# One attention layer and a gated MLP in split fp32: steps of the hand-written order moved, low parts kept in spare tiles

## The chip, the cores and the metric

The kernel runs on one core of one Trainium2 chip. The metric is device time in microseconds (us) of one execution, as the median of several runs. TensorE (PE) multiplies; VectorE (DVE), ScalarE (ACT) and GpSimd (POOL) do everything element by element; SyncE (SP) only starts transfers (DMA).

## What is computed

One layer of a decoder on an input of 1024 tokens by 1024 features: a dilated sliding-window attention and then a gated MLP, each on a normalised input and added to it. Cut to what runs:

```python
h = rms_norm(x, mixer_norm)                       # (1024, 1024)
proj = (h @ w_in).reshape(1, 1024, 3, 3, 8, 64)   # 3 groups; q, k, v; 8 heads of 64
for g, (window, dilation) in enumerate(((128, 1), (512, 4), (2048, 16))):
    q = rms_norm(proj[:, :, g, 0], q_gain[g]) * 64 ** -0.5
    k = rms_norm(proj[:, :, g, 1], k_gain[g])
    o, lse = dilated_window_attention(q, k, proj[:, :, g, 2], window, dilation)
weights = softmax(stack(lses), axis=0)            # over the 3 groups
x = x + sum(weights * stack(outs)).reshape(1, 1024, 512) @ w_out
u = causal_depthwise_conv(rms_norm(x, ffn_norm) @ w_up, conv_w, conv_b)   # width 3, 5632 channels
gate, up = split(u, 2)
x = x + (silu(gate) * up) @ w_down                # 2816 -> 1024
```

## The kernel before

**Products.** Each fp32 product is made of three fp32r products: every operand is split into a high part (a cast to fp32r, nearly always on ACT) and a low part (the operand less its high part, on DVE or POOL), and PE adds high x high, high x low and low x high into one PSUM bank. So each operand costs PE nothing before it is used, but one cast and one subtraction on the other engines.

**Attention.** Tokens are normalised in 8 blocks of 128 (`Normed`, L96): squares on ACT, the root on POOL, the scaling on DVE (L107), then 8 transposes on PE (`turn`, L109) whose result is split into `hh` (high) and `hl` (low), tiles of 9 places of [128, 1024]. The attention then runs in six units (group, half of its heads) in the order (2,0), (2,1), (1,0), (1,1), (0,0), (0,1), each over 8 blocks of 128 tokens: blocks 0 to 47. A block has 8 projection steps, one for each 128 features (`project`, three matmuls of 512 columns into `qk`; `project_v`, three of 256 into `vp`), and behind them its norm (squares on ACT, sums on DVE, roots on POOL), the scaling of its heads, the values (`values`, L223), transposes and splits of its heads, scores, softmax, and the product with the values. A unit needs 8 weight tiles of [128, 768]: `load_raw` starts the transfer, `load_w` (L176) makes the high part on ACT and the low part on DVE (tiles 0, 2, 4, 5, 7) or POOL (1, 3, 6). There are 11 places for split weights, so tiles 0 to 2 of a unit are split during the unit before, and tiles 3 to 7 around its last block.

Each group wants the tokens in another order. At the two unit boundaries where the group changes (ahead of blocks 16 and 32), `reorder` (L126) copies the 8 feature tiles of `hh` (on ACT and DVE in turn) and of `hl` (on POOL) into the new order. Copy k writes the place that copy k-1 has read (`slot0`, 9 places for 8 tiles), so all of them stand behind the last projection steps of the last block of the unit. In the first of these changes a copy is made in two instructions, in the second in four.

The masks of groups 1 and 0 are made once (`make_masks`, L422): three POOL instructions for positions, two transposes on PE, five instructions on DVE.

**MLP.** `out_project` (L547) multiplies the attention output by `w_out` (split in halves by `split_wo`), adds the residual, and `norm2` (L559) normalises; its last line writes the row block to memory through SP's queue. `turn2` transposes the rows to PSUM; `turned` copies them to SBUF on ACT. w_up is multiplied by a scheme with seven products where plain blocks take eight: of rows of even and odd number and of four sums of them (`even`, `odd`), with X, Y, Z and V, sums of the blocks of w_up. `even` splits even row blocks (blocks 0, 2 and 4 from their copy in SBUF, with the low part on POOL, block 6 from PSUM on DVE), `odd` makes and splits the sums. The 22 pairs of gate and up columns (`Pair`) are loaded (`load`), split (`first` for X, `sums` and `second` for Y, `third` for Z, `fourth` for V), multiplied (`product`), convolved (`conv`: ACT scales, two instructions of DVE, L732, add the other taps) and gated. The down product follows with the same scheme.

**Order.** PE, ACT, DVE and POOL run their instructions strictly in the order in which the program issues them. For attention and MLP input, `at(t, f)` enters each step with a number t, and the steps are issued sorted by t; block i's projection step k stands at 8 i + k, and what follows the block at 8 i + 8 plus the entries of `T` (L35); N = 384 is where the output product begins, and `t` from L796 on is the start of the last row block. The numbers are an order, not a time. Behind the plan, the pairs are written out line by line from L901 on. SP is ordered by the framework: a transfer is issued about when its buffer comes free, in the order of the program.

Buffers that the change touches: the tag `wraw` in pool A (4 places of [128, 1024]), which holds in turn tokens, two raw weight tiles, the mask positions and, behind the attention, the raw `w_out`.

## Time and profile before

| | before |
|---|---|
| median of 3 runs | 1334.71 us (1334.53 to 1338.65) |
| the profiled execution | 1336.1 us, of which the profile's span 1334.2 |
| mean granted clock of PE | 0.992 |
| PE busy | 1284.2 us, 96% |
| DVE busy | 901.2 us, 68% |
| ACT busy | 616.0 us, 46% |
| POOL busy | 495.9 us, 37% |

The profile is of one execution; its times count from the start of the span. An engine's busy time counts its instructions without branches, semaphores and the issue of transfers. Attention runs from 0 to about 604 us, the output product and the input of the MLP to about 720, the pairs to about 1117, and the down product to the end. A wait is the idle time of an engine ahead of an instruction, with the instruction that released it. "Granted clock" (PEclk) is the share of its full clock that PE was given in a stretch.

### The profile page before, as it was taken

How to read it: one execution, taken by the hardware profiler on the slowest of the kernel's cores; microseconds unless marked ns; L12 is line 12 of the kernel's file. 1: busy time of each engine (PE TensorE's matmuls, PEld its weight loads, DVE VectorE, ACT ScalarE, POOL GpSimd, SP SyncE). 2: the span in 40 equal slices, each digit the busy share in tenths (PEclk: the TensorE clock that was granted, in tenths of full speed). 3: DMA queues.
4: the chain of work that ended last, by engine and by line, in shares of the span. 5: the costliest groups of instructions: out<-in, count | busy, mean ns of one | idle time of the engine just before them, and what ended most of it. 6: DMA issues, size and time to landing. Idle time of an engine off the chain costs nothing.

```text
span 1334.2 us, 19243 instructions
## 1 busy us (share of the span) xinstructions
PE 1284.2 (96%) x6911; PEld 1078.4 (81%) x6911; DVE 901.2 (68%) x1544; ACT 616.0 (46%) x1277; POOL 495.9 (37%) x599
## 2 busy tenths in 40 slices
PE   6999998999999999999988999999999999999998
PEld 4898887888878888887766788888888887888887
DVE  4665455454564565556776898888888888876664
ACT  4655354444454444435544444444444536444442
POOL 4333345333354555454533554454454443000000
PEclk9999999999998999999999999999999999999999
DMA  7112212112111121113721333323332328973341
GB/s 240 41 64 75 86 37 72 34 48 61 48 46 35 51 58 50 31 39 122 227 77 39 94 104 111 102 82 100 118 115 83 111 71 283 348 250 105 95 143 64
DMA packets 111614, 132.16 MB, mean 99 GB/s; under 512 B 6126, under 2 KB 80030, under 8 KB 111518
## 3 DMA queue, kind: packets, MB, share of 16 engines
q1 hardware_dynamic: 111518, 130.93, 30.7%
q8 instruction: 55, 0.90, 0.3%
q14 instruction: 41, 0.34, 0.1%
HBM read 95.91 MB, written 35.00 MB: 98 GB/s over the span
## 4 chain that ended last, share of the span: by engine, by line
PE 43%; DVE 3%; issue 2%; DMA 1%; POOL 1%; ACT 1%; SPq 0%; DVEq 0%; POOLq 0%; ACTq 0%
PE ua L687 15%; PE y L871 15%; PE uc L687 8%; PE ub L687 4%; DVE c L732 1%; DMA wB<-in_ffn_w_down 1%; POOL wxl L518 0%; DMA graw<-gde 0%; ACT c L730 0%; DVE sz L660 0%; DVE sy L656 0%; DVE c L743 0%; DVE bt L598 0%; POOL wyl L518 0%; POOL wzl L518 0%
## 5 line engine op out<-in xcount | busy, mean ns | idle before, releaser
L871 PE MATMUL y<-wd,g 128*128 128x512 f32 x924 | 210.4, 389 | 0.2
L871 PEld LDWEIGHTS y<-wd,g 128*128 128x128 f32 x924 | 173.4, 188 | 36.9 <-DVE wd L598 0.6
L198 PE MATMUL qk<-w,hh 128*128 128x512 f32 x384 | 159.0, 414 | 0.5 <-ACT hh L115 0.5
L199 PE MATMUL qk<-w,hh 128*128 128x512 f32 x384 | 153.5, 400 | 0.0
L200 PE MATMUL qk<-w,hl 128*128 128x512 f32 x384 | 152.6, 397 | 0.5 <-DVE hl L116 0.5
L79 POOL TENSOR_SCALAR ms<-ss 128x8 f32<-128x8 f32 (+1 forms) x64 | 12.9, 201 | 312.9 <-DVE ss L216 265.9
L207 PE MATMUL vp<-w,hh 128*128 128x256 f32 x384 | 122.8, 320 | 3.6 <-DVE v L228 3.6
L732 DVE SCALAR_TENSOR_TENSOR c<-uu,cw,c 128x1023 f32<-128x1023 f32 (+1 forms) x44 | 95.6, 2174 | 38.3 <-ACT c L730 37.5
L209 PE MATMUL vp<-w,hl 128*128 128x256 f32 x384 | 108.8, 283 | 0.0
L208 PE MATMUL vp<-w,hh 128*128 128x256 f32 x384 | 108.8, 283 | 0.0
L518 POOL TENSOR_TENSOR wyl<-sy,wyh 128x1024 fp32r<-128x1024 f32 x21 | 56.5, 2689 | 115.0 <-issue 61.0
L80 POOL TENSOR_TENSOR rs<-ms,half 128x8 f32<-128x8 f32 (+1 forms) x64 | 87.5, 1367 | 5.4
L207 PEld LDWEIGHTS vp<-w,hh 128*128 128x128 f32 x384 | 73.5, 192 | 18.5 <-DVE v L228 5.8
L314 ACT ACTIVATE sm<-sm,ust 128x128 f32<-128x128 f32 (+1 forms) x128 | 53.4, 418 | 76.0 <-DVE ust L311 73.4
L200 PEld LDWEIGHTS qk<-w,hl 128*128 128x128 f32 x384 | 73.3, 191 | 18.7 <-DVE hl L116 1.2
L267 ACT ACTIVATE qT<-tr,gains 128x256 fp32r<-128x256 f32 x48 | 22.7, 473 | 134.8 <-PE tr L256 134.8
L216 DVE TENSOR_REDUCE ss<-qn 128x8 f32<-128x512 f32 x48 | 32.9, 685 | 75.8 <-ACT qn L214 75.8
L208 PEld LDWEIGHTS vp<-w,hh 128*128 128x128 f32 x384 | 73.6, 192 | 9.3
L270 DVE SCALAR_TENSOR_TENSOR qT<-tr,gains,qT 128x256 fp32r<-128x256 f32 x48 | 23.2, 484 | 85.5 <-ACT kT L269 85.5
L518 POOL TENSOR_TENSOR wxl<-uraw,wxh 128x1024 fp32r<-128x1024 f32 x22 | 58.4, 2653 | 44.8 <-ACT wxh L517 44.7
L198 PEld LDWEIGHTS qk<-w,hh 128*128 128x128 f32 x384 | 74.0, 193 | 1.1 <-ACT hh L115 0.9
L199 PEld LDWEIGHTS qk<-w,hh 128*128 128x128 f32 x384 | 74.1, 193 | 0.1
(186 smaller groups left out, 3363.0 us busy)
## 6 DMA issues: line engine op xcount, KB each, us to landing
uraw<-in_ffn_w_up SPq DMA_DIRECT2D x44, 512.0 KB
raw<-in_attn_w_in SPq DMA_DIRECT2D x48, 384.0 KB
wB<-in_ffn_w_down SPq DMA_DIRECT2D x44, 256.0 KB
graw<-gds SPq DMA_DIRECT2D x44, 256.0 KB
gdo<-c SPq DMA_DIRECT2D x11, 512.0 KB
...
```

What stands on the lines that cost most here:

```text
L80: nc.gpsimd.tensor_tensor(r[:, :n], t[:, :n], half[:, :n], op=ALU.pow)
L198: nc.tensor.matmul(self.qk, a, w[:, 0, :512], start=k == 0, stop=False)
L199: nc.tensor.matmul(self.qk, a, w[:, 1, :512], start=False, stop=False)
L200: nc.tensor.matmul(self.qk, b, w[:, 0, :512], start=False, stop=k == KT - 1)
L207: nc.tensor.matmul(self.vp, a, w[:, 0, 512:], start=k == 0, stop=False)
L208: nc.tensor.matmul(self.vp, a, w[:, 1, 512:], start=False, stop=False)
L209: nc.tensor.matmul(self.vp, b, w[:, 0, 512:], start=False, stop=k == KT - 1)
L314: nc.scalar.activation(sm[:, h, lo:], sm[:, h, lo:], AF.Exp, scale=-1.0, bias=st[:, 256 + h:257 + h], accum_out=st[:, 260 + h:261 + h])
L518: eng.tensor_sub(l, raw, h.bitcast(F32))
L687: nc.tensor.matmul(acc[:, lo:hi], w[z][:, s + k], a[y][:, j, k, lo:hi], start=begin and lo == 0 and k == 0 and n == 0, stop=k == 3 and n == 2,
L732: nc.vector.scalar_tensor_tensor(c[:, k:], u[:, :S - k], cw[:, 2 - k, j:j + 1], c[:, k:], op0=ALU.mult, op1=ALU.add)
L871: nc.tensor.matmul(y, gs[:, z, ts], ws[:, w], start=f and n == 0, stop=k == NK - 1 and n == 2, skip_group_check=True)
```

## The change

Nothing in what is computed changes; steps move in the order, some from one engine to another, and the low parts of reordered tokens get other places.

- **Start.** The load of the gain row and of five weight tiles is issued ahead of the tokens of block 1; the splits of the weights are ordered anew among the squares and scalings of blocks 0 and 1; the transposes of token block 1 go from 0.5 to 5.5, which is behind step 5 of block 0. `tp_gains` is parted: the four small loads stay at 2.5, the transpose goes to 8.3, behind block 0's steps.
- **Masks.** The three POOL instructions are split off (`mask_places`) and go to 76.8, the rest from 90 to 86.5.
- **Unit boundaries.** The high parts are copied in the same chain of places, while the low parts get places of their own (`places`): four of them in the first change of order tiles of tag `wraw`, the others places of `hl` that are free by then. The low copies k = 0 to 4 stand at -28, -23, -18, -13 and -8 against the start of the last block (t), the high copy 0 at t - 4.4, the others of both kinds from t + 2.62 on. Weight tiles 3 to 7 are split at 3.9, 8.7, 9.45, 10.6, 12.6 against t for units 2 and 4, at 3.9, 5.4, 8.7, 9.6, 10.8 for units 1, 3 and 5; the last block's values stand at 8.6.
- **Output weights.** The norm of block 47 goes 1.5 later, its values 0.3; the four first halves of `w_out` are split at N + 0.58 to 1.4, where they stood at 1.2 to 1.5, and tile 1's first half has its low part on DVE.
- **MLP input.** Row block 4 is split from PSUM like block 6, on DVE, and copied to SBUF later. In `odd` the cast and the split of the second half stand ahead of two of the sums. Steps 1 and 2 of `odd(5)` go 0.5 later, which sets the last residual's sum ahead of them. The second pair's X is split 2.8 later and on DVE, the third pair's X right behind the transposes of row block 7.
- **Pairs.** The third pair's first sums and Y are made ahead of the up half's convolution of the first pair.

```diff
@@ -34,7 +34,7 @@
...
-         fin=14.4, t0=4, so=1.2, so0=3.2, so1=3.3, so2=5.1, so3=5.2, to0=-3.43, to=-3.6, n2=3.0, n2s=5.8,
+         fin=14.4, t0=4, so0=3.2, so1=3.3, so2=5.1, so3=5.2, to0=-3.43, to=-3.6, n2=3.0, n2s=5.8,
@@ -117,29 +118,37 @@
-    slot0 = {2: 0, 1: 8, 0: 7}
-
-    def toks(g, t, k, c):
-
-        return t[:, (k + slot0[g]) % (KT + 1), c * P:(c + 1) * P]
-
-    def reorder(g, k):
-
-        for t, copy in ((hh, nc.scalar.copy if k % 2 else nc.vector.tensor_copy), (hl, nc.gpsimd.tensor_copy)):
-            src, dst = (t[:, (k + slot0[x]) % (KT + 1)] for x in (g + 1, g))
-            if g == 1:
-
-                src = src.rearrange("p (e r b n) -> p e r b n", e=2, r=4, b=2)
-                dst = dst.rearrange("p (r b e n) -> p e r b n", e=2, r=4, b=2)
+    places = {("h", 2): [*range(8)], ("h", 1): [8, *range(7)], ("h", 0): [7, 8, *range(6)],
+              ("l", 2): [*range(8)], ("l", 1): [8, "a", "b", "c", "d", 0, 1, 2],
+              ("l", 0): [3, 4, 5, 6, 7, 8, 0, 1]}
+    extra = {}
+
+    def place(z, g, k):
+        s = places[z, g][k]
+        return extra[s] if isinstance(s, str) else (hh if z == "h" else hl)[:, s]
+
+    def toks(g, z, k, c):
+
+        return place(z, g, k)[:, c * P:(c + 1) * P]
+
+    def reorder(g, z, k, copy):
+
+        if isinstance(places[z, g][k], str):
+            extra[places[z, g][k]] = A.tile([P, S], F32R, name="hx", tag="wraw", bufs=4)
+        src, dst = place(z, g + 1, k), place(z, g, k)
+        if g == 1:
+
+            src = src.rearrange("p (e r b n) -> p e r b n", e=2, r=4, b=2)
+            dst = dst.rearrange("p (r b e n) -> p e r b n", e=2, r=4, b=2)
+            for e in range(2):
+                copy(dst[:, e], src[:, e])
+        else:
+
+            src = src.rearrange("p (r b e c n) -> p b c e r n", r=4, b=2, e=2, c=4)
+            dst = dst.rearrange("p (b c e r n) -> p b c e r n", r=4, b=2, e=2, c=4)
+            for b in range(2):
                 for e in range(2):
-                    copy(dst[:, e], src[:, e])
-            else:
-
-                src = src.rearrange("p (r b e c n) -> p b c e r n", r=4, b=2, e=2, c=4)
-                dst = dst.rearrange("p (b c e r n) -> p b c e r n", r=4, b=2, e=2, c=4)
-                for b in range(2):
-                    for e in range(2):
-                        copy(dst[:, b, :, e], src[:, b, :, e])
+                    copy(dst[:, b, :, e], src[:, b, :, e])
 
     def rows(g, t, c):
 
...
@@ -409,57 +418,77 @@
     def first(i):
         xs[i] = Normed(i, xs[i])
 
-    def tp_gains():
-        grow = A.tile([P, 4, P], F32, name="grow", tag="qn", bufs=2)[:6, 0]
+    gr = {}
+
+    def load_gains():
+        gr[0] = grow = A.tile([P, 4, P], F32, name="grow", tag="qn", bufs=2)[:6, 0]
         for t in range(2):
             nc.sync.dma_start(grow[0:3, t * DH:(t + 1) * DH], q_gain)
             nc.sync.dma_start(grow[3:6, t * DH:(t + 1) * DH], k_gain)
+
+    def tp_gains():
+        grow = gr[0]
         tp = PA.tile([P, 512], F32, name="tp", tag="tr", bufs=2)
         nc.tensor.transpose(tp[:, :6], grow, ident[:6, :6])
         nc.vector.tensor_scalar(gains[:, 0:3], tp[:, 0:3], DH ** -0.5, None, op0=ALU.mult)
         nc.vector.tensor_copy(gains[:, 3:6], tp[:, 3:6])
 
-    def make_masks():
-        places = A.tile([P, 8, P], F32, name="kpos", tag="wraw", bufs=4)
-        kpos, kint = places[:, 0:2], places[:, 2:4].bitcast(I32)
+    kp = {}
+
+    def mask_places():
+        t = A.tile([P, 8, P], F32, name="kpos", tag="wraw", bufs=4)
+        kp[0] = kpos = t[:, 0:2]
+        kint = t[:, 2:4].bitcast(I32)
         nc.gpsimd.iota(kint[:, 0], pattern=[[1, 8], [8, 16]], base=0, channel_multiplier=0)
         nc.gpsimd.iota(kint[:, 1], pattern=[[1, 2], [2, 64]], base=0, channel_multiplier=0)
         nc.gpsimd.tensor_copy(kpos, kint)
-        kp = PA.tile([P, 4, P], F32, name="kp", tag="tr", bufs=2)
+
+    def make_masks():
+        kpos = kp[0]
...
     blocks = [Block(u, n) for u in range(6) for n in range(8)]
-    early = [(-20, -19.6, -19.35, -18), (-19.1, -17.8, -17.65, .5)]
+    early = [(-20, -19.2, -19.15, -18.9), (-19.3, -18.4, -18.2, 5.5)]
     for i in range(8):
         t = early[i] if i < 2 else (8 * i - 12, 8 * i + T["xf"], 8 * i + T["xs"], 8 * i + T["xt"])
         at(t[0], get_x, i)
         at(t[1], first, i)
         at(t[2], lambda i: xs[i].scale(), i)
         at(t[3], lambda i: xs[i].turn(0), i)
-        at(t[3] + .1, lambda i: xs[i].turn(1), i)
-    at(-19.4, get_gain)
-    at(2.5, tp_gains)
-    at(90, make_masks)
+        at(t[3] + .2, lambda i: xs[i].turn(1), i)
+    at(-19.9, get_gain)
+    at(2.5, load_gains)
+    at(8.3, tp_gains)
+    at(76.8, mask_places)
+    at(86.5, make_masks)
     for g, i in ((1, 16), (0, 32)):
-        for k in range(KT):
-            at(8 * (i - 1) + T["vs"] * (k - 1) + T["v"] + .02, reorder, g, k)
+        t = 8 * (i - 1)
+        at(t - 4.4, reorder, g, "h", 0, nc.scalar.copy)
+        for k in range(5):
+            at(t - 28 + 5 * k, reorder, g, "l", k, nc.gpsimd.tensor_copy)
+        for k, d in enumerate((2.62, 3.47, 4.6, 5.3, 6.1, 7.3, 8.65), 1):
+            at(t + d, reorder, g, "h", k, nc.scalar.copy if k % 2 else nc.vector.tensor_copy)
+        for k, d in enumerate((3.5, 5.3, 7.0) if g == 1 else (3.5, 7.2, 9), 5):
+            at(t + d, reorder, g, "l", k, nc.gpsimd.tensor_copy)
     SP = WA - KT
     for u in range(6):
         wt = {}
         for kt in range(KT):
             if u == 0:
-                t = lead = (-19.5, -19.3, -19.2)[kt] if kt < 3 else -18 + .1 * kt
+                t = (-19.1, -19, -18.8, -18.6, -18.5, -18.3, -18.1, -18)[kt]
+                lead = -19.8 + .1 * kt if kt < 5 else -18.7 + .05 * kt
             elif kt < SP:
                 t = 64 * u - 32 + T["wp"] + 4 * kt
                 lead = t - 3
             else:
-                t = 64 * u - KT + max((kt - SP) * T["vs"] + T["v"] + .01, kt - SP + T["w"])
+                t = 64 * u - KT + (3.9, *((8.7, 9.45, 10.6, 12.6) if u % 2 == 0 else (5.4, 8.7, 9.6, 10.8)))[kt - SP]
                 lead = max(t - 8, 64 * u - KT + (kt - SP - 3) * 1. + T["w"] + .5) if kt < SP + 3 else wt[kt - 3] + .3
             wt[kt] = t
             at(lead, load_raw, u, kt)
@@ -477,6 +506,8 @@
                 mw=(b.merge_weights,), a0=(b.attend, 0), a1=(b.attend, 1), mo=(b.merge_others,),
                 fin=(b.finish,)).items():
             late = not b.has_prev and (T["bd"] if name in ("sc", "sm") else T["bh"] if name in ("hT", "hs") else 0)
+            if b is blocks[-1] and name in ("norm", "val"):
+                late = 1.5 if name == "norm" else .3
             at(e + T[name] + late, step, *args)
 
 
@@ -520,7 +551,7 @@
 
     def split_wo(kt, hf):
         w = ring("wo", [P, 2, 512])
-        put([w[:, 0], w[:, 1]], M.wo[kt][:, hf * 512:(hf + 1) * 512], nc.gpsimd if kt == 1 else nc.vector)
+        put([w[:, 0], w[:, 1]], M.wo[kt][:, hf * 512:(hf + 1) * 512], nc.gpsimd if kt == 1 and hf else nc.vector)
         M.wo[kt, hf] = w
 
     def load_x1(i):
@@ -572,7 +603,7 @@
         for j in range(4):
             kt = 4 * q + j
             nc.tensor.transpose(pt[:, j], M.n2[i][:, kt * P:(kt + 1) * P], ident)
-        if i < 6 and i % 2 == 0 or i % 2 and q == 0:
+        if i < 4 and i % 2 == 0 or i % 2 and q == 0:
             turned(i, q)
 
     def turned(i, q):
@@ -599,7 +630,7 @@
 
     def even(i):
         c = slice(i // 2 * P, (i // 2 + 1) * P)
-        if i < 6:
+        if i < 4:
             put([b[:, :, :, c] for b in M.b1], M.h[i].rearrange("p (a k) t -> p a k t", a=2), nc.gpsimd)
         else:
             for q in range(2):
@@ -612,9 +643,9 @@
         if step == 0:
             x0, x1 = M.pt[i, 0], M.pt[i, 1]
             nc.vector.tensor_sub(e0, x0, e0)
+            put([b[:, 4, :, c] for b in M.bt], x1, nc.vector)
             nc.vector.tensor_sub(o0, x1, o0)
             nc.vector.tensor_sub(o1, x1, e0)
-            put([b[:, 4, :, c] for b in M.bt], x1, nc.vector)
             nc.vector.tensor_sub(e1, e1, o1)
         elif step == 1:
             put([b[:, 0:2, :, c] for b in M.bt], e.rearrange("p (a k) t -> p a k t", a=2), eng)
@@ -769,7 +800,7 @@
     at(N + .561, make_b1)
     for kt in range(4):
         at(N - 12, load_wo, kt)
-        at(N + T["so"] + .1 * kt, split_wo, kt, 0)
+        at(N + (.58, .59, 1, 1.4)[kt], split_wo, kt, 0)
         at(N + T[f"so{kt}"], split_wo, kt, 1)
     for i in range(8):
         t = N + T["t0"] + 6 * i
@@ -783,7 +814,7 @@
             continue
         for q in range(2):
             at(t + 9.2 + .1 * q, turn2, i, q)
-        if i == 6:
+        if i in (4, 6):
             at(t + 9.4, even, i)
             at(t + 12, turned, i, 0)
             at(t + 12.1, turned, i, 1)
@@ -791,8 +822,8 @@
             at(t + 12.2, even, i)
         else:
             at(t + 9.35, odd, i, 0)
-            at(t + 14.6, odd, i, 1, nc.gpsimd)
-            at(t + 14.7, odd, i, 2, nc.vector)
+            at(t + 14.6 + .5 * (i == 5), odd, i, 1, nc.gpsimd)
+            at(t + 14.7 + .5 * (i == 5), odd, i, 2, nc.vector)
     t = N + T["t0"] + 42
     at(N + 15, lambda: pa.__exit__(None, None, None))
     at(N + 15.1, make_bt)
@@ -801,7 +832,7 @@
     at(t - 12, pairs[0].load)
     at(t - 7.5, pairs[0].first)
     at(t - 4, pairs[1].load)
-    at(t + 3.1, pairs[1].first)
+    at(t + 5.9, pairs[1].first, nc.vector)
 
     def left_banks():
         pq.__exit__(None, None, None)
@@ -905,6 +936,7 @@
     p2.load()
     for q in range(2):
         turn2(7, q)
+    p2.first()
     p0.product(1, 384)
     odd(7, 0)
     p0.product(2, 384)
@@ -915,7 +947,6 @@
     odd(7, 1, onV)
     p1.product(1)
     odd(7, 2, onV)
-    p2.first()
     p1.product(2)
     p0.sums(0)
     p0.second(onV)
@@ -937,11 +968,11 @@
     p1.product(5)
     p0.product(4)
     p1.fourth()
+    p2.sums(0)
+    p2.second()
     p0.conv(True)
     p1.product(6)
-    p2.sums(0)
     p1.product(3)
-    p2.second()
     p0.gate()
     p3.load()
     p1.product(7)
```

## Rows read from the trace of the kernel before

**Rows 1.** The page's part 1: busy us (share of the span) x instructions.

```profile
PE 1284.2 (96%) x6911; PEld 1078.4 (81%) x6911; DVE 901.2 (68%) x1544; ACT 616.0 (46%) x1277; POOL 495.9 (37%) x599
```

**Rows 2.** Waits of PE, whole span: waiting <- releaser: us in total, times, longest.

```profile
PE xT L113 <- DVE xn L107: 11.9, 2, 9.0
PE xT L574 <- DVE xn L564: 6.8, 6, 2.7
PE pt L322 <- ACT sm L314: 6.4, 3, 3.1
PE vp L207 <- DVE v L228: 3.6, 5, 1.1
PE kp L430 <- POOL kpos L427: 3.0, 1, 3.0
...
PE uc L687 <- POOL wyl L518: 2.1, 1, 2.1
PE ua L687 <- POOL wxl L518: 1.8, 1, 1.8
```

**Rows 3.** Windows: us, PE, PEld, DVE, ACT, POOL busy (x), PEclk, DMA share, GB/s.

```profile
148.10:151.50 3.40, 3.40 (x13) 2.92 (x12) 1.52 (x6) 0.03 (x1) 0.02 (x1) 0.51 0.32 104
151.50:154.90 3.40, 3.40 (x27) 3.18 (x26) 0.59 (x2) 1.30 (x3) 0.00 (x0) 1.00 0.15 58
900.00:920.00 20.00, 20.00 (x88) 16.15 (x87) 17.45 (x15) 9.14 (x11) 10.28 (x5) 1.00 0.41 128
```

**Rows 4.** Timeline, start: start us, length us, instruction [idle before <- releaser].

```profile
16.90 1.94 PE L113 MATMUL xT<-ident,xn 128*128 128x128 f32 x8 [2.89 <-DVE xn L107]
17.00 0.83 ACT L179 CAST w<-raw 128x768 fp32r<-128x768 f32 x1 [0.23 <-DMA raw<-in_attn_w_in]
...
27.52 0.60 ACT L214 ACTIVATE qn<-qk 128x512 f32<-128x512 f32 x1 [7.01 <-PE qk L200]
```

**Rows 5.** Groups by shape, 186 to 222 us: xcount | busy us, mean ns | idle.

```profile
L135 POOL CAST hl<-hl 128x512 fp32r<-128x512 f32 x16 | 11.4, 741 | 0.4
...
L135 ACT CAST hh<-hh 128x512 fp32r<-128x512 f32 x8 | 4.6, 617 | 4.6 <-DVE hh L135 4.6
...
L179 ACT CAST w<-raw 128x768 fp32r<-128x768 f32 x5 | 4.1, 827 | 0.0
L180 DVE TENSOR_TENSOR w<-raw,w 128x768 fp32r<-128x768 f32 x3 | 3.0, 989 | 1.8 <-ACT w L179 1.8
```

**Rows 6.** Timeline of DVE, output weights and MLP input, 607 to 676 us.

```profile
607.43 2.22 DVE L598 TENSOR_TENSOR wo<-wraw,wo 128x512 fp32r<-128x512 f32 x2
...
665.16 3.37 DVE L564 SCALAR_TENSOR_TENSOR xn<-x,rs,gbc 128x1024 f32<-128x1024 f32 x1 [2.61 <-POOL rs L80]
...
674.83 1.29 DVE L564 SCALAR_TENSOR_TENSOR xn<-x,rs,gbc 128x1024 f32<-128x1024 f32 x1 [0.72 <-POOL rs L80]
```

**Rows 7.** Windows: boundaries of units 2 and 4, first output product.

```profile
200.00:220.00 20.00, 14.96 (x83) 12.44 (x84) 12.34 (x34) 8.92 (x26) 14.18 (x22) 0.91 0.34 112
380.00:400.00 20.00, 17.02 (x114) 14.42 (x112) 15.13 (x42) 12.37 (x32) 13.72 (x27) 1.00 0.22 69
400.00:420.00 20.00, 17.30 (x92) 14.46 (x93) 8.94 (x24) 9.12 (x31) 10.44 (x22) 0.83 0.17 52
600.00:620.00 20.00, 17.11 (x101) 13.01 (x99) 15.41 (x40) 11.01 (x30) 9.61 (x15) 0.91 0.29 99
```

**Rows 8.** Timeline of DVE, ACT and POOL in the first pairs, 720 to 735 us.

```profile
722.90 2.60 DVE L732 SCALAR_TENSOR_TENSOR c<-uu,cw,c 128x1023 f32<-128x1023 f32 x2 [5.08 <-ACT c L730]
...
726.86 1.04 ACT L517 CAST wyh<-sy 128x1024 fp32r<-128x1024 f32 x1 [3.52 <-DVE sy L657]
728.04 2.73 POOL L518 TENSOR_TENSOR wyl<-sy,wyh 128x1024 fp32r<-128x1024 f32 x1 [4.94 <-issue]
```

**Rows 9.** Windows: the first pairs.

```profile
720.00:740.00 20.00, 16.35 (x62) 12.20 (x61) 11.05 (x12) 10.27 (x14) 6.43 (x3) 0.91 0.18 56
740.00:800.00 60.00, 59.36 (x256) 47.59 (x255) 58.06 (x47) 27.64 (x35) 32.81 (x13) 1.00 0.35 110
```

9 lines of the change are left out of this document (5 added, 4 removed).

## The prediction

> **What bounds the kernel now.** The page's first part comes first: TensorE (PE) is busy 1284.2 us of a span of 1334.2 [rows 1], so for 50.0 us it does nothing, and the next question is who ends those waits. The view of PE's waits answers it [rows 2]: 11.9 us for the transposes of the attention input, 6.8 for those of the MLP input, 6.4 for softmax weights, 3.6 for the value buffer, 3.0 for the mask positions, 2.1 and 1.8 for weights split on GpSimd (POOL). Each row is a few long waits; the timeline gives their places. Last, the windows show a second price. In six stretches of 3.4 us behind such a wait (from 148.1, 206.1, 400.6, 410.9, 608.8 and 731.7 us on) PE is granted 0.5 of its clock, 1.2 instead of 2.4 GHz; 13 matmuls are done in the first of them and 27 in the same time behind it [rows 3], so each costs about 3.4 / 2 = 1.7 us, six of them 10.2. What can be won is at most 50 + 10.2 us, with the start and the end of the kernel in it. So I go through the change stage by stage: which of these waits it ends, and what is late next.
>
> **The start (A).** The transposes of token block 1 stand ahead of step 1 of attention block 0, and PE waits 2.9 us for them until 16.90; block 0's last score projection ends at 27.5 (ACT takes it up at 27.52) [rows 4]. The change sets steps 1 to 5 of block 0 ahead of those transposes. Loads: the gain row and five weight tiles go ahead of block 1's tokens, but the bytes are the same, so the last weight tile still lands at 17.0, where its cast waits for the DMA [rows 4]. Casts follow the loads. A matmul of 512 columns takes 20 / 88 = 0.23 us from 900 on [rows 3], so a step of three 0.7, or 1.4 at half clock, and steps 0 to 5 with the first values are done by about 18 us. Left are 8 transposes (PE needed 1.9 us for them at 16.90 [rows 4]), steps 6 and 7, and their values: 4 us. The last low part is ready at 17.0 + 0.83 (cast) + 0.99 (subtraction) [rows 5], or 1.29 later behind the scaling of a block [rows 6]: 18.8 to 20.1. Block 0 ends near 22.5 instead of 27.5: I take 4.8 us; 3 if PE stays at 1.2 GHz to its end, 6.5 if the low part comes early. The gains' four small loads keep their place on SP's queue; their transpose, now behind block 0, finds them landed.
>
> **The masks (B).** PE waits 3.0 us for three POOL instructions that stand behind a block's normalisation [rows 2]. They move ahead by 13 steps, where POOL is idle. The wait goes, with the stretch from 148.1 on that follows it: 3.0 + 1.7 = 4.7. The five VectorE (DVE) instructions that make the masks now lie ahead of one softmax; for that I leave 0.2: 4.5 (3.0 to 4.7).
>
> **Odd units (C).** At units 1, 3 and 5 the splits of weight tiles 5 to 7 leave the last block's window and follow its values, for which PE waited: 3.6 us in five waits [rows 2], three of them here (2.2). I take 1.8 (0.5 to 2.2), since in the next block's window those engines have idle time.
>
> **The boundaries of units 2 and 4 (D, E).** Around the first of them the old order has 16 copies on POOL (11.4 us), 8 on DVE, 8 on ScalarE (ACT; 4.6 us) and five weight casts [rows 5]. Copy k+1 writes the place that copy k reads, so DVE and ACT wait for each other (4.6 us of ACT's idle time), and the softmax of block 14 stands behind both: PE's longest wait of its row, 3.1 us [rows 2]. From 200 to 220 PE is idle 20 - 14.96 = 5.0 us and loses 1.7 to the clock [rows 7]. The change moves five of eight low copies 5 steps apart into earlier blocks (four spare tiles make this possible) and three or four of the splits behind the last block's values. ACT then has one copy ahead of block 14's exponentials, DVE one copy and a sum; the wait of 3.1 shrinks to about 0.5. New waits come up: the value buffer (0.3); the low part of tile 4, whose cast (0.83) and subtraction (0.99) now follow a copy of 2 x 0.62 [rows 5] and end some 0.7 us after PE asks; and the heads of block 15, whose scaling now stands behind tile 5's subtraction (1.0). Unit 2: 5.0 + 1.7 - 2.5 = 4.2, bounds 1 and 7. At unit 4 PE is idle 3.0 + 2.7 us, and the clock of 0.83 is two stretches, 3.4 [rows 7]; the same new waits stay, about 2.4: 5.7 + 3.4 - 2.4 = 6.7, bounds 2 and 9. The output weights can now load only when the spare tiles are free, at the end of unit 3; they are used behind block 47, two units later: nothing.
>
> **Output weights (F).** In the first output product PE is idle 2.9 us of 20 and loses 1.7 to the clock [rows 7]. The low parts of tiles 2 and 3 take DVE 2.22 us beside POOL's [rows 6]; now DVE makes all four, ahead of the last block's norm, which it delays. The waits get other owners, of about the same length; the product ends some 1.7 us earlier (0 to 3.5).
>
> **The MLP's input (G).** Of the 6.8 us [rows 2], 2.7 are one wait: the scaling of row block 5 takes 3.37 us beside POOL's split of block 4, another takes 1.29 [rows 6]. That split now reads PSUM, on DVE, at a time in which DVE is idle: 2.1 gained. The casts ahead of the sums free ACT for the next block's squares two subtractions earlier, and the last residual goes ahead of block 5's splits; that ends most of the other five waits, 4.1 us, of which I take 3.2. G = 5.3 (3 to 7). On SP's queue the third pair's load stands behind the write of that residual, so it comes earlier too, and the cast that now stands ahead of block 7's finds it landed. The two rows say that DVE beside POOL is the price. The Trainium skill ("SBUF — State Buffer", "Who interferes with whom") has it that a DVE instruction with two SBUF inputs contends with a POOL instruction that reads SBUF, and one with a single SBUF input doesn't; by it the split from PSUM is never slowed. If the 3.37 us had another cause, G would be 3.2 and the result 1304.
>
> **The pairs (H).** PE's 1.8 us for the third pair's first low part go, since it is made some 9 us earlier. The third pair's sums move into DVE's idle time, 5.08 us up to 722.90; their low part, 2.73 us on POOL from 728.04, can then be ready before PE asks [rows 8]. That ends most of 3.6 idle us from 720 to 740, with one stretch at half clock [rows 9]: 1.8 + 3.5 + 1.7 = 7.0. But behind 740 DVE is busy 58.06 us of 60 [rows 9], so PE can keep no more than DVE's own work moves forward: the 5.08 us less the cast (1.04) that now stands ahead of the up half's taps on ACT [rows 8], 4.0. I take 3.8 (1.8 to 7).
>
> **Sum.** 4.8 + 4.5 + 1.8 + 4.2 + 6.7 + 1.7 + 5.3 + 3.8 = 32.8. The profiled execution took 1336.1 us (its span and 1.9 around it), so it would take 1303.3; the median of the runs is 1.4 below it: 1302. Its own range is 1294 to 1309.
>
> **Rivals.** *The waits move on at the boundaries.* ACT and DVE run in order; if the splits behind the last block's values hold up softmax and heads as the copies did, and the three half-clock stretches (5.1) stay, D + E give 2.9 instead of 10.9: 1310. For it: the three new waits. Against: 16 POOL copies become 6, and one copy instead of three stands ahead of the first softmax. *DVE becomes the bound.* It gets the splits of block 4 and of the second pair, over 1 us each, at the end of the MLP's input, and is full behind 740: H gives nothing and G 3.0: 1302 + 3.8 + 2.3 = 1308. For it: 58.06 of 60. Against: the idle 5.08 us just ahead. Both together: 1316. *The steps move and their producers don't*, loads and normalisations being as late as before: only A and B stay, 1334.7 - 9.3 = 1325. *Slower: the loop over pairs settles where POOL and DVE collide.* From 900 to 920 DVE is busy 17.45 us of 20 [rows 3]; in a collision an instruction of 1.29 takes 3.37, 2.1 more [rows 6]. The loop is entered with other phases than before. With two collisions more in each 20 us (4.2) DVE needs 21.7, and 19 pairs give 19 x 1.7 = 32; with a third now and then 38: 1302 + 38 = 1340. It decides from 1.75 us per pair on. Against: from 740 to 800 the phases are as bad as that, and PE is still busy 59.36 of 60. The skill's page named above says that the second of two such instructions blocks for the whole of the first, which would make a collision as long as POOL's instruction.
>
> **How the numbers follow.** Forecast 0.60; the boundaries alone 0.17; DVE, alone or with them, 0.11; steps without their producers 0.04; gains and new waits that cancel, within 0.3% of before (about what a measurement of this kernel can tell from no change), 0.04; slower 0.04. The range reaches from 1293 (D, E and H near their good ends) to 1318 (both middle rivals, and 2 us of the unknown costs). Faster by over 0.3%: 0.92; same 0.04; slower 0.04.
>
> **What would show it.** Right: no PE wait for the mask positions or for the third pair's first low parts; block 0 ends near 22.5; the waits for softmax at both boundaries are under 1 us, with no half clock there; the scaling of row block 5 is near 1.3 us; PE still waits 1 to 2 us behind 735 for the third pair. Wrong: half clock at both boundaries; the third pair's cast waiting for its load; DVE at 20 of 20 us in the loop.

## The result, and the profile after

The changed kernel takes **1301.95 us** (median of 4 runs, 1301.71 to 1302.57) against 1335.76 of the kernel before beside it (1334.53 to 1338.65): a ratio of 0.9745, 95% interval 0.9727 to 0.9762. Forecast were 1302, from 1293 to 1318. The profiled span is 1300.0 us where it was 1334.2. The first part of the page after, which answers to [rows 1]:

```profile
PE 1274.2 (98%) x6911; PEld 1071.0 (82%) x6911; DVE 896.2 (69%) x1542; ACT 617.1 (47%) x1284; POOL 486.7 (37%) x596
```

Of the 34.2 us, TensorE's busy time gives 10.0 (1284.2 to 1274.2, with the same 6911 matmuls; none of the six stretches at half clock is left), its idle time 24.2 (50.0 to 25.8). PE's waits after, which answer to [rows 2]:

```profile
PE xT L114 <- DVE xn L108: 8.8, 1, 8.8
PE tr L265 <- DVE qn L229: 2.9, 5, 0.9
PE uc L718 <- ACT p L741: 1.3, 1, 1.3
PE pt L331 <- ACT sm L323: 1.2, 2, 0.9
...
PE xT L605 <- DVE xn L595: 0.9, 2, 0.5
...
```

The columns are those of [rows 2]. The waits for the masks are gone, the 3.6 us for the value buffer as good as gone (0.2), the softmax's 6.4 are 1.2, those for the MLP's input 0.9 instead of 6.8. One row has grown, the heads (`tr`): 2.9 us in five waits, one at each of the five unit boundaries, where before there were two waits, 2.3 us. The first experiments are about it.

**Where the time went, stage by stage.** Both kernels run the same steps on PE, so the start of one instruction in both traces measures all that was gained up to it. Marks are the squares that ACT takes of a block's scores behind its last projection step (block 0: 27.52 us in [rows 4]), and in the MLP a sum on DVE that empties PE's bank. Block 0's mark after, and the transposes of token block 1:

```profile
18.73 1.07 PE L114 MATMUL xT<-ident,xn 128*128 128x128 f32 x8
...
22.15 0.60 ACT L223 ACTIVATE qn<-qk 128x512 f32<-128x512 f32 x1 [0.62 <-PE qk L209]
```

| stage, and the mark that ends it | before | after | gained here | forecast |
|---|---|---|---|---|
| A start, squares of block 5 | 86.11 | 81.08 | 5.03 | 4.8 |
| C unit 1, block 9 | 131.89 | 126.78 | 0.08 | 0.6 |
| B masks, block 12 | 169.43 | 159.79 | 4.53 | 4.5 |
| D boundary of unit 2, block 18 | 243.12 | 228.36 | 5.12 | 4.2 |
| C unit 3, block 28 | 361.20 | 346.50 | -0.06 | 0.6 |
| E boundary of unit 4, block 34 | 441.49 | 418.51 | 8.28 | 6.7 |
| C unit 5, block 45 | 578.82 | 555.87 | -0.03 | 0.6 |
| F output weights, fourth sum of a residual | 628.33 | 604.51 | 0.87 | 1.7 |
| G input of the MLP, second bank sum (`ug`) of the pairs | 693.36 | 662.32 | 7.22 | 5.3 |
| H pairs, last of these bank sums | 1114.66 | 1080.74 | 2.88 | 3.8 |
| together | | | 33.9 | 32.8 |

The same stages in the windows of both traces (columns as in [rows 3]); here B, D, E, F and G before:

```profile
131.89:169.43 37.54, 34.55 (x214) 30.54 (x213) 17.98 (x57) 15.18 (x47) 11.35 (x22) 0.95 0.25 79
169.43:243.12 73.69, 68.24 (x432) 59.48 (x430) 41.03 (x113) 35.74 (x104) 33.40 (x54) 0.98 0.15 50
...
373.14:441.49 68.35, 62.67 (x397) 54.03 (x396) 37.98 (x105) 31.94 (x94) 36.62 (x72) 0.95 0.13 41
...
578.82:628.33 49.51, 46.45 (x292) 38.51 (x291) 31.44 (x78) 22.61 (x62) 23.68 (x47) 0.97 0.25 84
628.33:693.36 65.03, 57.56 (x313) 47.40 (x312) 47.00 (x57) 34.70 (x53) 31.31 (x25) 1.00 0.53 169
```

and after:

```profile
126.78:159.79 33.01, 33.01 (x214) 29.21 (x213) 17.87 (x57) 15.02 (x48) 13.95 (x25) 1.00 0.09 26
159.79:228.36 68.57, 67.17 (x431) 58.22 (x430) 38.79 (x111) 36.48 (x105) 28.00 (x48) 1.00 0.18 54
...
358.47:418.51 60.04, 58.87 (x397) 51.34 (x396) 34.54 (x101) 33.07 (x98) 29.69 (x56) 1.00 0.26 82
...
555.87:604.51 48.64, 45.19 (x292) 37.38 (x291) 31.45 (x80) 22.85 (x63) 23.38 (x46) 1.00 0.26 86
604.51:662.32 57.81, 56.67 (x313) 47.93 (x312) 46.89 (x60) 34.66 (x54) 25.57 (x23) 1.00 0.60 190
```

Length less PE's busy time is idle time; the change of the busy time at the same number of matmuls (in D one fewer) is mostly the clock. B: 2.99 us idle and 1.54 of clock are gone. D: idle 5.45 to 1.40, clock 1.07. E: idle 5.68 to 1.17, clock 3.80. F: idle 3.06 to 3.45, clock 1.26. G: idle 7.47 to 1.14, and 0.89 less busy time, though the granted clock is full in both windows; where that part comes from was not followed.

Of the 10.0 us of busy time, 8.6 stand in the five stages that lost a stretch at half clock (B, D, E, F, and 0.91 in H). In A it is 1.12 (73.20 to 72.08): PE's first matmuls of 512 columns start 0.43 us apart, the later ones 0.23, and the faster ones begin at 22.1 us before and at 15.4 after.

The sum is off by 1.1 us in 33.9. That is partly luck: C, F and H gave 3.6 us less than forecast, D, E and G 4.4 more, A and B 0.3. The experiments ask why.

### The profile page after: what moved, and what is told of

It is laid out like the page before. It is cut to its first block, busy times and chain, and to the rows that moved or that the text cites. A ratio compares the mean times of both kernels' runs of the same rounds, so it can differ in the third digit from the quotient of the medians.

```text
span 1300.0 us, 19219 instructions
## 1 busy us (share of the span) xinstructions
PE 1274.2 (98%) x6911; PEld 1071.0 (82%) x6911; DVE 896.2 (69%) x1542; ACT 617.1 (47%) x1284; POOL 486.7 (37%) x596
## 4 chain that ended last, share of the span: by engine, by line
PE 43%; DVE 4%; ACT 2%; issue 1%; DMA 1%; POOL 0%; SPq 0%; DVEq 0%; POOLq 0%; ACTq 0%
PE y L902 15%; PE ua L718 15%; PE uc L718 8%; PE ub L718 4%; DVE c L763 2%; ACT c L761 1%; DMA x<-in_x 1%; DMA graw<-gde 0%; DVE bt L629 0%; DVE sz L691 0%; DVE c L774 0%; DVE xn L595 0%; DMA wB<-in_ffn_w_down 0%; DVE sy L687 0%; POOL b L629 0%
## 5 line engine op out<-in xcount | busy, mean ns | idle before, releaser
L209 PE MATMUL qk<-w,hl 128*128 128x512 f32 x320 | 126.1, 394 | 0.0
L218 PE MATMUL vp<-w,hl 128*128 128x256 f32 x320 | 90.0, 281 | 0.0
L320 DVE CUSTOM_DVE_ANT_0 sm<-s,mask 128x128 f32<-128x128 f32 (+1 forms) x192 | 56.0, 347 | 24.0 <-PE s L298 18.5
L209 PEld LDWEIGHTS qk<-w,hl 128*128 128x128 f32 x320 | 60.5, 189 | 14.6 <-DVE hl L117 0.2
```

The lines of the kernel that those rows point to most:

```text
L209: nc.tensor.matmul(self.qk, b, w[:, 0, :512], start=False, stop=k == KT - 1)
L218: nc.tensor.matmul(self.vp, b, w[:, 0, 512:], start=False, stop=k == KT - 1)
L320: nc.vector.tensor_tensor_reduce(out=sm[:, h, lo:], in0=src[h], in1=m, op0=ALU.add, op1=ALU.min, scale=-1.0, scalar=3e38, accum_out=st[:, ...
```

## Experiments

Each is the changed kernel with one edit (the last joins two), so it is read against 1301.95 us and the marks above. Of a long line of code only the part that differs is shown. The medians of the kernel before, run beside them, moved from 1335.8 to 1338.6 us, so a small difference between two medians says little, and the marks are the better measure. In kernels that do not touch a stage, the gains of B, C, D, E and H repeat within 0.15 us, and so do those of F but for one run (see the end). Two stages vary more: A gained 5.03 to 5.60 us in the twelve kernels with the same start, and G 6.23 to 7.22 where nothing in it was edited.

**Odd units as before.**

```diff
-(3.9, *((8.7, 9.45, 10.6, 12.6) if u % 2 == 0 else (5.4, 8.7, 9.6, 10.8)))
+(3.9 if u % 2 == 0 else 3.1, *((8.7, 9.45, 10.6, 12.6) if u % 2 == 0 else (4.1, 5.1, 6.1, 7.1)))
```

> The changed kernel with one part undone: at units 1, 3 and 5 weight tiles 3 to 7 are split at their old places, ahead of the last block's values. Theory from the trace after (the removed waits for the value buffer came back as later heads and a later second softmax part): the time stays, 1302 +- 0.5, with three waits of the value buffer of 1.1, 0.7 and 0.4 us back and those of the heads (0.44, 0.40, 0.49) gone. Rival, the prediction's term: the part is worth 1.8 us and the time rises to about 1303.8.

Measured: 1302.55 us (1301.97 to 1302.93). Stages C gained -0.02, -0.11 and 0.01 us where the change had 0.08, -0.06 and -0.03. PE's waits in this run:

```profile
PE vp L216 <- DVE v L237: 2.4, 4, 1.1
PE tr L265 <- DVE qn L229: 1.6, 2, 0.9
```

The three waits for the value buffer are back, those for the heads at the odd units gone, and the time is the same to 0.1 us per unit. Part C traded one wait for another. What made the new one stands in the timelines (start, length, instruction, idle time before). Unit 1 in the kernel before:

```profile
112.14 1.64 POOL L80 TENSOR_TENSOR rs<-ms,half 128x8 f32<-128x8 f32 x1
...
112.16 0.39 PE L207 MATMUL vp<-w,hh 128*128 128x256 f32 x1 [1.11 <-DVE v L228]
```

and the same place in the changed kernel:

```profile
106.08 0.96 DVE L189 TENSOR_TENSOR w<-raw,w 128x768 fp32r<-128x768 f32 x1
106.14 2.40 POOL L80 TENSOR_TENSOR rs<-ms,half 128x8 f32<-128x8 f32 x1
...
108.51 1.81 POOL L189 TENSOR_TENSOR w<-raw,w 128x768 fp32r<-128x768 f32 x1
108.57 0.69 DVE L229 TENSOR_TENSOR qn<-qk,rs 128x512 f32<-128x512 f32 x1 [1.20 <-POOL rs L80]
109.18 1.96 DVE L189 TENSOR_TENSOR w<-raw,w 128x768 fp32r<-128x768 f32 x1
...
109.32 0.66 PE L265 MATMUL tr<-ident,qn 128*128 128x128 f32 x4 [0.44 <-DVE qn L229]
```

DVE's subtraction for tile 5 begins 0.06 us ahead of POOL's root, and the root takes 2.40 us instead of 1.64; the scaling of the heads waits for it, and PE for the scaling. Then tile 7's subtraction lies beside POOL's for tile 6 and takes 1.96 us instead of 0.96, and holds the low half of the softmax weights behind it (`pT`), for which PE waits another 0.08 us. PE's idle time in this stage is 0.66 us where it was 1.11, but its busy time is 0.37 longer at the same 290 matmuls, for a reason that was not followed.

At unit 3 it is the same (the root takes 2.39 us from 289.17 on), but not at unit 5. There POOL's root begins first, at 483.09, and takes its 1.64; what holds the scaling is a small subtraction on DVE ahead of it, which takes 1.72 us beside POOL's split of tile 6 and 0.17 in its 15 other places:

```profile
484.69 1.83 POOL L189 TENSOR_TENSOR w<-raw,w 128x768 fp32r<-128x768 f32 x1
...
484.82 1.72 DVE L372 TENSOR_TENSOR e<-nm,mt 128x12 f32<-128x12 f32 x1
```

**Tile 5 behind the scaling.**

```diff
-(8.7, 9.45, 10.6, 12.6) if u % 2 == 0 else (5.4, 8.7, 9.6, 10.8)
+(8.7, 10.55, 10.6, 12.6) if u % 2 == 0 else (5.4, 10.55, 10.6, 10.8)
```

> The changed kernel with one more move: at every unit boundary tile 5 is split behind the scaling of the last block's heads (10.55) and not ahead of it (8.7 or 9.45). Theory: what holds the heads is that one subtraction on DVE, which stands ahead of the scaling and, at odd units, stretches the root on GpSimd beside it (2.40 us against 1.64); then the five waits of TensorE for the heads (0.44, 0.70, 0.40, 0.92, 0.49) go and the kernel gains 2.5 to 3 us: 1299 to 1299.5. Rival: the splits are late wherever they stand, and the next thing in line (the second softmax part, tiles 6 and 7) takes over: 0 to 0.5 us, 1301.5 to 1302.

Measured: 1303.72 us (1302.27 to 1303.83), slower. Against the change, units 1, 2, 3 and 5 lost 0.12, 0.26, 0.30 and 0.30 us, unit 4 gained 0.28; another 1.0 was lost in stage G (below). The waits for the heads are gone as expected, but tile 5 is late itself, here at unit 2:

```profile
198.29 1.82 POOL L189 TENSOR_TENSOR w<-raw,w 128x768 fp32r<-128x768 f32 x1 [1.12 <-ACT w L188]
198.31 2.62 DVE L189 TENSOR_TENSOR w<-raw,w 128x768 fp32r<-128x768 f32 x1
...
200.99 0.50 PE L208 MATMUL qk<-w,hh 128*128 128x512 f32 x1 [1.29 <-DVE w L189]
```

The theory fell in its second half: moving a subtraction out of the way was not enough, as it now met POOL's. It started 0.02 us behind it and took 2.62 us: POOL's 1.82 first, and then its own 0.8 to 0.96. Without the meeting it would have ended at 199.3, ahead of PE.

**Tile 5 on POOL, tile 6 on DVE**, so that the two do not meet and no subtraction of DVE stands ahead of the scaling:

```diff
-(nc.vector if kt in (0, 2, 4, 5, 7) else nc.gpsimd)
+(nc.vector if kt in ((0, 2, 4, 6, 7) if u else (0, 2, 4, 5, 7)) else nc.gpsimd)
...
-(8.7, 9.45, 10.6, 12.6) if u % 2 == 0 else (5.4, 8.7, 9.6, 10.8)
+(8.7, 9.45, 11.96, 12.6) if u % 2 == 0 else (5.4, 8.7, 11.96, 12.6)
```

> The changed kernel with the low parts of tiles 5 and 6 of units 1 to 5 exchanged between engines: tile 5 on GpSimd right behind the root (GpSimd has nothing else then), tile 6 on DVE behind the scaling of the heads and the second softmax part. Theory from the run in which tile 5 went behind the scaling: there the subtraction took 2.62 us instead of 0.96, as GpSimd's split of tile 6 lay beside it, and only that made tile 5 late. Without a DVE subtraction ahead of the scaling and without that meeting, the five waits for the heads (2.95 us together) go and nothing takes their place: 1299 to 1300. Rival: the last weight tiles simply come too late for these engines, a wait for tile 5 or 6 takes the place, and the time is 1302 or more.

Measured: 1300.52 us (1300.04 to 1301.49). That is 0.5 above the range that was expected. The odd units gained 0.52, 0.61 and 0.70 us against before, unit 2 5.97 (0.85 more than the change), unit 4 7.51 (0.77 less), and stage G gave 0.78 less than with the change (see the third pair's load below). The theory holds at four boundaries, though at unit 1 two subtractions still meet (DVE's takes 1.65 us from 108.55 on); PE waits for neither. The edit also sets tile 6, and at the odd units tile 7, later. At unit 4 POOL still makes a low copy (1.81 us from 383.38 on) ahead of the split, and the rival came true:

```profile
385.15 2.53 POOL L189 TENSOR_TENSOR w<-raw,w 128x768 fp32r<-128x768 f32 x1
...
387.74 0.50 PE L208 MATMUL qk<-w,hh 128*128 128x512 f32 x1 [1.61 <-POOL w L189]
```

**Low copies late.**

```diff
-at(t - 28 + 5 * k, reorder, g, "l", k, nc.gpsimd.tensor_copy)
+at(t + 1.77 + .85 * k, reorder, g, "l", k, nc.gpsimd.tensor_copy)
...
-(3.5, 5.3, 7.0) if g == 1 else (3.5, 7.2, 9)
+(6.02, 6.87, 7.72) if g == 1 else (6.02, 7.2, 9)
```

> The changed kernel with the low copies of both changes of token order made late again, all eight from t + 1.77 on; places, high copies and splits of weights stay as changed. Theory: the early low copies free GpSimd for the root and the splits, and without them units 2 and 4 lose at least half of their 5.1 and 8.3 us: 1307 to 1312. Rival: the boundary was set by ACT and DVE (splits ahead of the softmax), the copies on GpSimd lie beside it, and the time stays within 1 us of 1302.

Measured: 1306.68 us (1305.91 to 1307.63). D gained 1.86 us instead of 5.12, E 5.91 instead of 8.28: 5.6 less, a little under the expected 6.7 (half of 13.4), and far from the rival. From 201.5 to 204.8 us the granted clock is 0.50.

**Splits of units 2 and 4 early.**

```diff
-(3.9, *((8.7, 9.45, 10.6, 12.6) if u % 2 == 0 else (5.4, 8.7, 9.6, 10.8)))
+(3.1, *((4.1, 5.1, 6.1, 7.1) if u % 2 == 0 else (5.4, 8.7, 9.6, 10.8)))
```

> The changed kernel with the splits of tiles 3 to 7 of units 2 and 4 at their old places (3.1 to 7.1), ahead of the last block's values and among the copies; the low copies stay early. Theory: ACT and DVE have five casts and three subtractions more ahead of block 14's and block 30's exponentials, so the wait for softmax weights comes back at 1 to 3 us each with a stretch of half clock: 1304 to 1311. Rival: with the low copies out of the way there is room for both, and the time stays within 1 us of 1302.

Measured: 1310.40 us (1308.95 to 1311.50). D gained 2.37, E 2.99: 8.0 less than the change. As expected, half clock is back at both boundaries (0.50 from 195.0 to 198.3 and from 392.9 to 396.2 us). PE's waits with late copies:

```profile
PE pt L331 <- ACT sm L323: 3.6, 3, 1.4
```

and with early splits:

```profile
PE pt L331 <- ACT sm L323: 4.5, 3, 2.2
PE vp L216 <- DVE v L237: 3.2, 2, 2.4
```

The waits for softmax, 6.4 us before [rows 2] and 1.2 with the change, come back in part in both. The two halves of D and E cost 5.6 and 8.0 us when they are taken out one at a time, 13.7 together, and the stages gained 13.4. So they seem to add up, though no run takes out both, and the splits are the larger half, while the prediction spent most of its words on the copies.

**Transposes of token block 1 early again.**

```diff
-early = [(-20, -19.2, -19.15, -18.9), (-19.3, -18.4, -18.2, 5.5)]
+early = [(-20, -19.2, -19.15, -18.9), (-19.3, -18.4, -18.2, .5)]
...
-at(t[3] + .2, lambda i: xs[i].turn(1), i)
+at(t[3] + .1, lambda i: xs[i].turn(1), i)
```

> The changed kernel with the transposes of token block 1 at their old place, ahead of step 1 of block 0; loads, splits and scalings stay as changed. Theory (the prediction's): the steps set ahead of those transposes are the gain, TensorE waits for block 1's scaling until about 18.5 us and block 0 ends 5 to 7 us later than 22.15: 1306.5 to 1309. Rival: the new order of loads and splits is the gain, the place of the transposes hardly matters: within 1 us of 1302.

Measured: 1309.55 us (1308.26 to 1309.78), half a microsecond above the expected range; the profiled execution is the one of 1308.26, 6.3 above that of the changed kernel. Block 0's mark is at 28.38 us, 6.2 later than with the change and 0.9 later than before, as the waits for the scaling of tokens (`xT`) show:

```profile
PE xT L114 <- DVE xn L108: 14.4, 2, 8.3
```

14.4 less the first 8.3 is a wait of 6.1 us for block 1, whose tokens now load behind five weight tiles. So the steps ahead of the transposes are the gain, and the new order of loads and splits alone gains nothing: it costs about 1 us, not much more than stage A varies.

**Row block 4 on POOL again.**

```diff
-        if i < 4 and i % 2 == 0 or i % 2 and q == 0:
+        if i < 6 and i % 2 == 0 or i % 2 and q == 0:
...
-        if i < 4:
+        if i < 6:
...
-        if i in (4, 6):
+        if i == 6:
```

> The changed kernel with row block 4 split as before: copied to SBUF at once, its low part made on GpSimd from the copy. Theory: that GpSimd subtraction lies beside the scaling of row block 5, which takes 3.4 us again where it takes 1.28, and TensorE waits about 2 us more: 1304 (1303.5 to 1305). Rival: with the last residual ahead of block 5's splits the two no longer meet, or the wait is taken out of another one: within 0.7 us of 1302.

Measured: 1304.54 us (1304.20 to 1304.70); stage G gained 4.01 us instead of 7.22. In its timeline the two instructions of [rows 6] are back with the durations of before:

```profile
638.74 2.36 POOL L629 TENSOR_TENSOR b<-h,b 128x1024 fp32r<-128x1024 f32 x1
638.81 3.37 DVE L595 SCALAR_TENSOR_TENSOR xn<-x,rs,gbc 128x1024 f32<-128x1024 f32 x1 [2.94 <-POOL rs L80]
...
642.23 1.11 PE L605 MATMUL xT<-ident,xn 128*128 128x128 f32 x7 [2.51 <-DVE xn L595]
```

and here the scaling of row block 5 in the changed kernel:

```profile
639.10 1.28 DVE L595 SCALAR_TENSOR_TENSOR xn<-x,rs,gbc 128x1024 f32<-128x1024 f32 x1 [1.74 <-POOL rs L80]
```

The cause of the longer scaling is shown: 3.37 us beside POOL's split, 1.28 without. The 3.2 us are not all its price, though. PE's idle time in stage G is 2.78 us instead of 1.14, which is 1.64 more; the other 1.57 are busy time, since here a stretch at half clock follows the wait of 2.51:

```profile
643.00:646.30 3.30, 3.30 (x11) 2.66 (x9) 3.25 (x6) 2.20 (x4) 0.74 (x2) 0.50 0.55 220
```

In the kernel before, the same wait (2.7 us, ahead of 668.6) is followed by no such stretch, so against that kernel the 1.64 us are the better measure, not far from the 2.1 forecast.

**Old order in the odd row blocks.**

```diff
+            nc.vector.tensor_sub(o0, x1, o0)
+            nc.vector.tensor_sub(o1, x1, e0)
             put([b[:, 4, :, c] for b in M.bt], x1, nc.vector)
-            nc.vector.tensor_sub(o0, x1, o0)
-            nc.vector.tensor_sub(o1, x1, e0)
...
-at(t + 14.6 + .5 * (i == 5), odd, i, 1, nc.gpsimd)
-at(t + 14.7 + .5 * (i == 5), odd, i, 2, nc.vector)
+at(t + 14.6, odd, i, 1, nc.gpsimd)
+at(t + 14.7, odd, i, 2, nc.vector)
```

> The changed kernel with the old order in the odd row blocks: both sums ahead of the cast and split of the second half, and block 5's splits ahead of the last residual's sum. The prediction's term: these two end most of the five smaller waits for the MLP's input and are worth 3.2 us: 1305.2. Rival: block 4's split from PSUM did the work, and the order is worth under 1 us: 1302 to 1303.

Measured: 1306.72 us (1306.58 to 1307.47); stage G gained 2.31 us instead of 7.22 (PE's idle time there is 4.94 instead of 1.14), so the order is worth 4.9, and the rival falls. Which of the two moves does it was not asked apart. Six waits for the MLP's input are back:

```profile
PE xT L605 <- DVE xn L595: 4.2, 6, 1.1
```

**The third pair's sums late again.**

```diff
-    p2.sums(0)
-    p2.second()
     p0.conv(True)
     p1.product(6)
+    p2.sums(0)
     p1.product(3)
+    p2.second()
```

> The changed kernel with the third pair's sums and Y behind the up half's taps of the first pair again; its X stays early. Three answers differ. The prediction's term (3.8 less the 1.8 for X): 2.0 us lost, 1304. The marks in the two traces (between the third pair's first sum and the loop the lead grows from 33.07 to 33.91 only): 0.8 us lost, 1302.8. The waits of before alone (1.32 + 2.13 and one stretch of half clock, 1.7), if nothing behind them gives any of it back: 5.2 us lost, 1307.

Measured: 1303.73 us (1302.62 to 1304.04); stage H gained 1.53 us instead of 2.88. Both waits of before are back in PE's timeline, and from 698 to 701 us the window shows half clock:

```profile
694.98 0.73 PE L718 MATMUL uc<-bt,wyh 128*128 128x512 f32 x2 [1.33 <-ACT wyh L548]
697.84 0.80 PE L718 MATMUL uc<-bt,wyl 128*128 128x512 f32 x1 [2.13 <-POOL wyl L549]
```

```profile
698.00:701.00 3.00, 3.00 (x8) 2.33 (x8) 2.93 (x4) 0.00 (x0) 0.00 (x0) 0.50 0.00 0
```

Those 3.46 us and the stretch cost 1.35 in the end. PE's idle time in stage H grew by 0.14 us only (4.10 to 4.24) and its busy time by 1.21 (414.32 to 415.53): the waits that the changed kernel has there (0.50 for a copy on ACT, 1.29 for the copy of the third pair's fifth product, 0.69 for the fourth pair's X, 0.44 for a sum on DVE) do not occur in this run. That agrees with the cap that the prediction worked out from DVE's 58.06 busy us of 60, which is tighter than the 2.0 forecast for this part.

A second sign that PE does not set the pace there: in four other runs (tile 5 behind the scaling, splits early, tile 5 on POOL, transposes early) a stretch at half clock falls among the first pairs (0.50 from 706.9 to 710.2 us in the first of them), and stage H still gained 2.80 to 2.87 us.

**The third pair's X behind the cast of row block 7.**

```diff
-    p2.first()
     p0.product(1, 384)
     odd(7, 0)
+    p2.first()
```

> The changed kernel with the third pair's X one place later on ACT, behind the cast of row block 7's second half. In four other runs of such kernels that cast came 0 to 1.1 us late, as the DMA of the third pair's weights was its releaser, and TensorE then waited 0.27 to 1.21 us for the first pair's sum. Theory: X ahead of block 7's cast is what puts a transfer on the path; moved behind, the wait goes and the time falls by 0.3 to 1.3 us, 1300.7 to 1301.7, with less spread. Rival: X is then late itself, and TensorE waits for its low part as it did before the change (1.79 us): 1302.5 to 1303.5.

Measured: 1303.05 us (1302.83 to 1303.18), slower; stage G gained 5.89 us. The theory fell, and not by its rival either, although the time lies in the rival's range: what PE waits for is the first pair's sum. The timeline of POOL, DVE and PE in this run:

```profile
656.51 2.38 POOL L549 TENSOR_TENSOR wxl<-uraw,wxh 128x1024 fp32r<-128x1024 f32 x1 [6.34 <-ACT wxh L548]
656.72 0.68 DVE L648 TENSOR_TENSOR h<-xT,h 128x512 f32<-128x512 f32 x1
657.44 2.01 DVE L649 TENSOR_TENSOR h<-h 128x512 f32<-128x512 f32 x1
...
660.10 0.73 PE L718 MATMUL ub<-b,wxh 128*128 128x512 f32 x2 [1.59 <-DVE ug L738]
```

and in the changed kernel:

```profile
654.77 2.39 POOL L549 TENSOR_TENSOR wxl<-uraw,wxh 128x1024 fp32r<-128x1024 f32 x1 [4.13 <-ACT wxh L548]
...
656.60 0.68 DVE L647 TENSOR_TENSOR h<-xT,h 128x512 f32<-128x512 f32 x1
...
657.91 0.69 DVE L649 TENSOR_TENSOR h<-h 128x512 f32<-128x512 f32 x1
...
659.26 0.73 PE L718 MATMUL ub<-b,wxh 128*128 128x512 f32 x2 [0.27 <-DVE ug L738]
```

In the changed kernel POOL's split lies beside the sums that read PSUM (`xT`), which take their 0.68 us as ever. 1.7 us later it lies beside the last sum, whose inputs are both in SBUF: 2.01 us instead of 0.69, and PE waits 1.3 us longer. This is the rule that the prediction took from the Trainium skill ("SBUF — State Buffer", "Who interferes with whom"), with both of its cases in one place: the trace agrees, 0.68 with one SBUF input, 2.01 with two.

**The third pair's load earlier.**

```diff
+    at(t + 5.7, pairs[2].load)
...
-    p2.load()
```

> The changed kernel with the third pair's load issued ahead of the last residual's write instead of behind it. Theory: the load, issued at 648.3 us, is what makes the third pair's cast late by 0 to 1.1 us from run to run; issued earlier, no cast waits for a DMA there, the first pair's sum is late by 0.27 us at most, the spread of the runs shrinks, and the median falls by 0 to 0.5 us: 1301.5 to 1302. Rival: its buffers come free only then, the queue holds the residual's write and the load at the same place, and nothing changes (1302.0 with the same spread).

Measured: 1301.67 us (1301.64 to 1302.80). The cast, at 653.21, waits for no transfer in this run. In the run with tile 5 behind the scaling it did:

```profile
655.51 1.05 ACT L548 CAST wxh<-uraw 128x1024 fp32r<-128x1024 f32 x1 [1.14 <-DMA uraw<-in_ffn_w_up]
```

In the profile of the changed kernel it waited for none either, so this one profile does not show that the early load is the reason; with the load behind the write, eight of nine other profiles had such a wait, with the early load neither of two. Of the rest of the expectation, PE's wait for the first pair's sum is 0.27, but the spread of the runs did not shrink and the median is where it was. What a late transfer costs shows in stage G: 6.23 us gained instead of 7.22 where the cast waited 1.14, 6.44 where it waited 0.96, 6.89 where it waited 0.54.

**Both improvements together**: the exchange at units 1, 2, 3 and 5, and the early load.

```diff
-(nc.vector if kt in (0, 2, 4, 5, 7) else nc.gpsimd)
+(nc.vector if kt in ((0, 2, 4, 5, 7) if u in (0, 4) else (0, 2, 4, 6, 7)) else nc.gpsimd)
...
-(8.7, 9.45, 10.6, 12.6) if u % 2 == 0 else (5.4, 8.7, 9.6, 10.8)
+(8.7, 9.45, 10.6, 12.6) if u == 4 else (8.7, 9.45, 11.96, 12.6) if u == 2 else (5.4, 8.7, 11.96, 12.6)
...
+    at(t + 5.7, pairs[2].load)
...
-    p2.load()
```

> The changed kernel with tile 5 on GpSimd and tile 6 on DVE at units 1, 2, 3 and 5 (at unit 4, where GpSimd still has low copies to make and tile 5 came 1.61 us late, it stays as changed), and with the third pair's load ahead of the last residual's write. Sum of the marks: 0.44 + 0.85 + 0.67 + 0.73 = 2.7 us earlier at the end of the attention, and no late transfer behind it: 1299.0 to 1299.5. Rival: with another phase at the MLP's input the gain is given back, as 0.8 of it was in the run with the exchange alone: 1300 to 1300.5.

Measured: 1299.10 us (1299.04 to 1300.37), a ratio to before of 0.9712 (0.9699 to 0.9726) and 2.9 us under the changed kernel. Units 1, 2, 3 and 5 gained 0.52, 5.95, 0.60 and 0.70 us, unit 4 8.25, stage G 7.17. It is the fastest of all.

## Why the prediction came out, step by step

- **The bound** (idle time and half clock, 50 + 10.2): right. What was gained is 24.2 us of idle time and 10.0 of busy time, 8.6 of these in the stages that lost their half clock.
- **A**, 4.8 forecast, 5.03 measured (up to 5.60 in other runs): right, and for the reason given: with the transposes back, 6.2 us are lost. Block 0 ended at 22.15 (22.5 said). One term was too long: the 8 transposes took 1.07 us and not 1.9, as PE had reached its faster rate by then.
- **B**, 4.5 and 4.53: right; 2.99 idle and 1.54 of clock. No run undoes this part alone; the wait and the half clock that it was to end are gone.
- **C**, 1.8 and 0.0: wrong. The step that failed is "in the next block's window those engines have idle time". They have, but not ahead of the scaling of the heads: at units 1 and 3 the root met tile 5's subtraction, at unit 5 a small subtraction on DVE met tile 6's on POOL, and at each of the three units 0.4 to 0.5 us went to the heads. Idle time in these stages fell from 2.23 to 1.64 us, but busy time rose by as much (0.6, at one matmul more); why it rose stays open.
- **D, E**, 4.2 and 6.7 against 5.12 and 8.28: mechanism right, size off. The mis-sized term is the new waits, 2.5 and 2.4 forecast; PE idles 1.40 and 1.17 us in those windows. D's half-clock stretch gave 1.07 instead of 1.7, E's two 3.80 instead of 3.4.
- **F**, 1.7 and 0.87: "other owners, of about the same length" was too kind; idle time rose from 3.06 to 3.45, and the clock gave 1.26. No run undoes this part, so which of its moves did what is not shown.
- **G**, 5.3 and 7.22: mechanism right, one part larger than said: the order was worth 4.9 (3.2 forecast). Taking back block 4's split cost 3.2 (2.1 forecast), but half of that is a stretch at half clock that the kernel before does not have there. That is why the two come to more than the 7.22 gained.
- **H**, 3.8 and 2.88: the cap was right and binds a little harder. The third pair's sums are worth 1.35. That the third pair's load "landed" was true by a hair: in eight of the nine other profiles that have load and cast in these places, the cast waited for it, 0.25 to 1.14 us.
- **The rivals.** The boundaries' waits did move on, at the odd units. DVE did bound the first pairs (busy 58.29 us of the 60 from 706 on, and in four runs a half-clock stretch there cost stage H under 0.1 us), but G kept its gain. The loop over the pairs kept its pace: from the seventh of the bank sums on to the last of 44, the lead stays between 33.91 and 33.94 us, so the slower rival had nothing to it here.
- What was said to show it: no wait for mask positions, softmax waits under 1 us, block 5's scaling at 1.28, all as stated. PE's waits for the third pair came as 1.29 and 0.27 us at 704 to 705.
